# Decoder block: four-pair scans, placement copies on ScalarE, fewer VectorE steps per table, longer rows in the first loads

## Chip, cores and metric

The kernel runs on one core of one Trainium2 chip. The metric is device time in microseconds of one execution; a kernel is timed in several runs, and the median of the three runs before the change is 398.58 us (397.07 to 398.76). The engines are named as the profile names them: PE is TensorE (matmuls), PEld its weight loads, DVE is VectorE, ACT is ScalarE, POOL is GpSimd and SP is the queue from which all loads of weights are issued.

## The reference

One layer of a decoder block over 256 tokens of width 1024, in float32. Two branches run in parallel on the same projections: block-sparse attention (with a block of 256 tokens it is plain causal attention over 8 heads of 64) and an S5 diagonal state-space branch. Both are gated, summed, projected and normalized, and a convolutional gated FFN with a second normalization follows.

```python
proj = h @ w_in[l]                                  # q, k, v, u, g_attn, g_ssm
q, k = apply_partial_rotary(q), apply_partial_rotary(k)
attn = moba_attention(q, k, v)
ssm = s5_branch(u, a_re, a_im, log_dt, b_re, b_im, c_re, c_im, d, w_glu)
merged = sigmoid(g_attn) * (attn @ w_attn_proj) + sigmoid(g_ssm) * (ssm @ w_ssm_proj)
h = layer_norm(ALPHA * h + merged @ w_out, ln1_g, ln1_b)
val, gate = split(causal_depthwise_conv(h @ w_up, conv_w, conv_b))
h = layer_norm(ALPHA * h + (gelu(gate) * val) @ w_down, ln2_g, ln2_b)
```

The S5 branch has 32 groups of 16 channels with 64 complex states each. With `dt = exp(log_dt)` the state decays by `lb = exp(a * dt)` per token:

```python
x = z * (b @ u)                      # z from lb, a: complex, per state
h[s] = lb * h[s - 1] + x[s]          # over 256 tokens
y = Re(c @ h) + d * u
y = gelu(y);  y = y * sigmoid(y @ w_glu)
```

## The kernel before

**Order.** The program first records every operation with its reads, its writes and an estimated cost (class Recorder, lines 100 to 281). It then plans the order of each engine's queue by a list schedule over these costs, forward and backward, and issues all operations in the order that the planner found best. Every engine works through its queue in that order. The cost of an instruction comes from its class (Vec line 284, Act 351, Pe 377, Dma 425); a DMA is reckoned at its bytes by 330 GB/s (line 431). So a change of any cost or operation can change the whole order.

**Weights.** Products run in a reduced float32 form, so each operand is split into a high and a low part. A chunk of 128 x 1024 weights (512 KB) is loaded from the SP queue into a ring of `raw` buffers (three at first; `ctab` and `stab` are added later, line 979). ACT copies the high part to `wh` (some of the buffers are `yhl`, `shl`, `athl`, `xh`), DVE subtracts it from `raw` and writes the low part `wl` (`split_to`, line 476). A product is then three matmuls: high x high, low x high, high x low (`three`, line 491). A `raw` buffer can be loaded again only when DVE has made the low part.

**Start.** Before the first weights PE runs 28 small matmuls on zeros. `x` comes transposed in pieces (`x_piece`, line 562) into `gt`; the four chunks of the u weights go in halves to `ctab`, `stab` and two parts of `el`, and PE multiplies them unsplit (lines 579 to 591), into the banks `u_acc`. `small` is a tensor of parameters, of which the first 48 columns come early. Then come the q, k, v chunks and 16 gate chunks.

**S5 constants.** On 128 x 16 tiles (states of two groups by 16 pairs of groups) DVE works out exponentials, sine and cosine by series that run as scans (lines 624 to 696), then `z`, the even powers and the squared decay `mag2`. Two consecutive tokens are taken as one step of 128 (`NCH`). `uc` holds u in even and odd tokens: 32 copies of 32 rows out of the PSUM banks (lines 699 to 705), half on ACT, half on DVE. `e_tilde` and `gamma` (lines 728 and 738) build the input and output operands `et` and `gm` out of two products each on 128 x 512, and a sum per half of 64 rows, which writes to interleaved columns. `toeplitz` (841) builds the part within a step, `tz`.

**Tables and scans.** The rotation of the state is taken out of the scan: `turn_parts` makes angles in turns, and `tables(un)` (line 777) for a unit of four pairs adds a coarse and a fine angle, takes away the nearest whole number, and takes a sine and, through the absolute value, a cosine on ACT. `ssm_unit` (line 866) then multiplies by the tables, scans with the real decay (a scan for each of four pairs, real and imaginary, lines 885 to 888) and multiplies back. `ssm_out` (896) makes the outputs and applies Gelu. The four units are interleaved with the four pairs of attention heads and the gates (lines 976 to 983).

**After it.** Projections of attention and S5 output, the GLU product, the output projection, the first normalization, then 22 blocks of the FFN (from line 1159) and the second normalization with the output.

Of the kernel before, what the change touches and what calls it, by code (L numbers as in the profile page):

```python
# [20 lines left out]
P = 128  # L21
# [53 lines left out]
def _free(ap):  # L75
    n = 1
    for d in ap.shape[1:]:
        n *= d
    return n
# [345 lines left out]
class Dma:  # L425
# [2 lines left out]

    def dma_start(self, o, a):
        sb_in, sb_out = a.space != bass.MemoryType.DRAM, o.space != bass.MemoryType.DRAM  # L430
        n = _free(o if sb_out else a) * P * 4
        self.rec.add("SP", lambda: self.real.dma_start(o, a), [o] if sb_out else [],  # L432
                     [a] if sb_in else [], 0.45, dur=n / 330e3)

# [1 line left out]
def block_kernel(ctx: ExitStack, tc: tile.TileContext, w, xtok, small, lnv, out):  # L438
# [73 lines left out]
    qk = Ring([sb(f"qk{i}", NH, DH) for i in range(2)])  # L512
    ra, rb = sb("ra", NH, 16), sb("rb", NH, 16)
    sa, sb_, sc, sd = (sb(n, 4, NCH) for n in ("sa", "sb", "sc", "sd"))
    sgr, sgi = sb("sgr", 4, NCH), sb("sgi", 4, NCH)
    ga, gb, gk = (sb(n, 4, NCH) for n in ("ga", "gb", "gk"))
    hri = [(sb(f"hr{i}", 4, NCH + 1), sb(f"hi{i}", 4, NCH + 1)) for i in range(2)]
# [27 lines left out]
        return sml[:, a:b]  # L545

    eye = col("eye")
    halfpi = sb("halfpi", 1)

    warm = sb("warm", P, dt=BF16)  # L550
    V.memset(warm, 0.0)
    G.memset(halfpi, math.pi / 2)


    late = [tuple(again(t[:, i], (1024,)) for i in range(2)) for t in (yhl, shl, athl)]
# [6 lines left out]
    def x_piece(k0, k1):  # L562
        SP.dma_start(again(xr, (KD * S,))[:, k0 * S:k1 * S], w[C_X + k0 // 4][:, k0 % 4 * S:((k1 - 1) % 4 + 1) * S])

    x_piece(0, 1)


    A.copy(xh[:, 0, 0:1], warm[:, 0:1])
# [9 lines left out]
    u_room = [again(ctab, (1024,)), again(stab, (1024,))] + [again(el[:, 4 * i:4 * i + 4], (1024,)) for i in range(2)]  # L578
    for kk in range(4):
        r = u_room[kk]  # L580
        for j, (n0, n1) in enumerate(((0, 512), (512, 1024))):
            SP.dma_start(r[:, n0:n1], w[C_U + kk][:, n0:n1])
            if kk == 0 and j == 0:
                x_piece(1, 2)
            elif kk < 3 and j == 1:
                x_piece(2 * kk + 2, 2 * kk + 4)
        if kk == 0:
            SP.dma_start(sml[:, 0:48], small[:, 0:48])
        for h in range(2):
            for m in range(4):  # L590
                u_sum[m].add(r[:, h * 512 + m * P:h * 512 + (m + 1) * P], xr[:, 2 * kk + h])
# [107 lines left out]
    for q in range(4):  # L699
        for i4 in range(4):  # L700
            i = 4 * q + i4
            for j in range(2):
                b0 = 64 * (i % 2) + 32 * j
                src = u_acc[q][32 * i4:32 * i4 + 32, j:S:2]
                (V.tensor_copy if q % 2 else A.copy)(uc[b0:b0 + 32, i // 2], src)

# [1 line left out]
        G.memset(et[ri], 0.0)  # L710
    G.memset(gm, 0.0)
    G.memset(tz, 0.0)
    for t in hri[0] + hri[1]:
        G.memset(t[:, :, 0:1], 0.0)

# [12 lines left out]
    def e_tilde(ri, t0, t1_):  # L728

        b0, b1, op = ((bre, bim, SU), (bim, bre, AD))[ri]  # L730
        a, b = again(t0, ikh), again(t1_, ikh)
        tt(a, bc_h(zz[:, 0::2, 0]), bc_k(b0), MU)
        tt(b, bc_h(zz[:, 0::2, 1]), bc_k(b1), MU)
        for g in range(2):
            r = slice(64 * g, 64 * g + 64)
            tt(et[ri][r, :, :, g], a[r], b[r], op)

    def gamma(ri):

        b0, b1 = ((cre, cim), (cim, cre))[ri]  # L740
        cc = (zz[:, 1::2], zn)[ri]
        a, b = again(ga, ikh), again(gb, ikh)
        tt(a, bc_h(cc[:, :, 0]), bc_k(b0), MU)
        tt(b, bc_h(cc[:, :, 1]), bc_k(b1), MU)
        for g in range(2):
            r = slice(64 * g, 64 * g + 64)
            tt(gm[r, ri, :, 1:3, g], a[r], b[r], AD if ri else SU)

    for g in range(2):
        r = slice(64 * g, 64 * g + 64)  # L750
# [11 lines left out]
    def turn_parts():  # L762
        tt(whole, cidx, bc_c(tau), MU)
        ts(whole, whole, MAGIC, AD, MAGIC, SU)
        tt(turns, cidx, bc_c(tau_h), MU)
        tt(part, cidx, bc_c(tau_l), MU)
        tt(turns, turns, whole, SU)
        tt(turns, turns, part, AD)


    b0 = _COLS["bre"][0]
# [5 lines left out]
    def tables(un):  # L777
        tab = slice(8 * (un // 2) + un % 2, 8 * (un // 2) + 8, 2)
        tt(again(ga, (4, 8, 16)), turns[:, tab, 0:8].unsqueeze(3).to_broadcast([P, 4, 8, 16]),
           turns[:, tab, 8:24].unsqueeze(2).to_broadcast([P, 4, 8, 16]), AD)  # L780
        ts(gk, ga, MAGIC, AD, MAGIC, SU)
        tt(ga, ga, gk, SU)
        ct, st = cs[un]
        A.activation(st, ga, AF.Sin, scale=6.283185)
        V.tensor_scalar(gk.bitcast(I32), ga.bitcast(I32), 0x7FFFFFFF, None, op0=ALU.bitwise_and)
        A.activation(ct, gk, AF.Sin, scale=-6.283185, bias=halfpi)

    turn_parts()
    tables(0)
    e_tilde(0, sa, sb_)  # L790
    e_tilde(1, ga, gb)
    gamma(0)
    gamma(1)
    tables(1)
    tables(2)

# [46 lines left out]
    def toeplitz(half):  # L843
        pt = s5()
        for mm in range(4):
            m = 4 * half + mm
            e = er()
            for ri in range(2):
                A.copy(e[:, ri], et[ri][:, 2 * m:2 * m + 2, 1].rearrange("p i g h -> p i (g h)")
                       .unsqueeze(2).to_broadcast([P, 2, 2, 32]))  # L850
            for ri in range(2):
                T.matmul(pt[:, mm * P:(mm + 1) * P], e[:, ri].rearrange("p i j c -> p (i j c)"),
                         gm[:, ri, 2 * m:2 * m + 2, 0:2].rearrange("p i m g h -> p i (m g h)"),
                         start=ri == 0, stop=ri == 1)
        pv = pt.rearrange("p (a i m c) -> p a i m c", a=4, i=2, m=2)
        ms = slice(4 * half, 4 * half + 4)
        for par in range(2):
            r0 = slice(64 * par, 64 * par + 32)
            r1 = slice(64 * par + 32, 64 * par + 64)
            tt(tz[r0, ms, 0:32], pv[r0, :, par, 0], di[r0, ms], AD)  # L860
            V.tensor_copy(tz[r0, ms, 32:64], pv[r0, :, par, 1])
            tt(tz[r1, ms, 32:64], pv[r1, :, par, 0], di[r1, ms], AD)

    y = again(et[0], (4, S))
# [1 line left out]
    def ssm_unit(un):  # L866

        big, par = un // 2, un % 2
        pairs = [8 * big + 2 * k + par for k in range(4)]
        r = slice(64 * par, 64 * par + 64)  # L870
        pe = [s5(), s5()]
        for ri in range(2):
            for k, i in enumerate(pairs):
                T.matmul(pe[ri][:, k * P:(k + 1) * P], el[r, i // 2, ri], uc[r, i // 2],
                         start=True, stop=True)
        er_, ei_ = (p.rearrange("p (a c) -> p a c", a=4) for p in pe)
        ct, st = cs[un]
        hr_, hi_ = hri[par]
        tt(sa, ct, er_, MU)
        tt(sd, st, er_, MU)  # L880
        tt(sb_, st, ei_, MU)
        tt(sc, ct, ei_, MU)
        tt(sa, sa, sb_, AD)
        tt(sc, sc, sd, SU)
        for src, dst in ((sa, sgr), (sc, sgi)):
            for k, i in enumerate(pairs):
                V.tensor_tensor_scan(dst[:, k], mag2[:, i:i + 1].to_broadcast([P, NCH]),
                                     src[:, k], 0.0, MU, AD)
        tt(ga, ct, sgi, MU)
        tt(gb, st, sgr, MU)  # L890
        tt(hi_[:, :, 1:], ga, gb, AD)
        tt(sa, ct, sgr, MU)
        tt(sb_, st, sgi, MU)
        tt(hr_[:, :, 1:], sa, sb_, SU)
# [375 lines left out]
```

## Time and profile before

| | us |
|---|---|
| median of three runs | 398.58 |
| profiled execution | 399.22 |
| its span in the trace | 397.1 |
| PE busy in the span | 378.6 |
| DVE busy | 325.3 |
| ACT busy | 225.2 |
| POOL busy | 7.0 |

The span runs from the first to the last instruction of the execution; the profiled execution's own time holds some 2 us around it. A busy share of an engine is an average over stages that have different limits. A busy PE is one that has a matmul in flight: records overlap, so the spacing of their starts tells how fast it works. In rows of a timeline, the numbers are the start, the time, the engine, the line, the operation, what it writes and reads, and the count of merged instructions; in brackets stands the idle time before it and what ended that. Nearly all DVE rows have line 295, all ACT rows 371 and all DMA issues 432, as those are the lines of the recording helpers, so the tiles tell them apart.

### The profile page before, as it was taken

The numbers are of one execution on the slowest core, as the hardware profiler recorded it, in microseconds if no ns is written. First come the engines' busy times: TensorE is split into PE (matmuls) and PEld (weight loads), VectorE is DVE, ScalarE is ACT, GpSimd is POOL, SyncE is SP. The second block draws the span as 40 slices with busy tenths as digits, with TensorE's granted clock in tenths as the row PEclk, the third lists the DMA queues.
The fourth block names the chain that finished last, engine by engine and source line by source line (L and its number), as shares of the span: only waits on it lengthen the run. The fifth ranks groups of instructions, "written<-read, shape, count | busy, mean of one in ns | idle before, by whom it ended". The sixth has DMA issues, their size and how long they took to land.

```text
span 397.1 us, 6974 instructions
## 1 busy us (share of the span) xinstructions
PE 378.6 (95%) x2668; PEld 341.8 (86%) x2668; DVE 325.3 (82%) x636; ACT 225.2 (57%) x405; POOL 7.0 (2%) x47
## 2 busy tenths in 40 slices
PE   9898999999999999999799999999999999999980
PEld 8676787899798989988799999999999999999960
DVE  3899999899889967987988997777777677776666
ACT  3476585764897549724427756565665656555400
POOL 6000000000000000000000000000000000000000
PEclk9999999999999999999989999999999999999996
DMA  7814506364811663578327776554556555552002
GB/s 209 354 53 158 194 19 210 110 210 155 273 54 54 214 213 106 200 267 301 135 65 269 249 227 210 205 206 163 196 177 211 186 189 179 193 194 71 2 0 106
DMA packets 19905, 67.36 MB, mean 170 GB/s; under 512 B 2336, under 2 KB 2848, under 8 KB 19872
## 3 DMA queue, kind: packets, MB, share of 16 engines
q1 hardware_dynamic: 19872, 66.91, 49.3%
q8 instruction: 21, 0.34, 0.4%
q14 instruction: 12, 0.10, 0.1%
HBM read 65.86 MB, written 1.05 MB: 168 GB/s over the span
## 4 chain that ended last, share of the span: by engine, by line
PE 78%; DVE 14%; DMA 3%; issue 2%; SPq 1%; ACT 1%; DVEq 0%; ACTq 0%
PE bank L390 68%; PE bank L409 5%; DVE gm L295 3%; PE bank L416 3%; DMA ctab<-w 2%; DVE wl L295 2%; DMA gt<-w 2%; PE bank L422 1%; DVE uc L295 1%; DVE st L295 1%; DVE ty L295 1%; SPq L432 1%; DVE xl L295 1%; DVE ga L295 1%; DVE et L295 1%
## 5 line engine op out<-in xcount | busy, mean ns | idle before, releaser
L295 DVE TENSOR_TENSOR wl<-raw,wh 128x1024 fp32r<-128x1024 f32 x52 | 63.0, 1219 | 5.3 <-ACT wh L371 5.2
L295 DVE SCALAR_TENSOR_TENSOR qk<-bank,sml,qk 128x255 f32<-128x255 f32 (+1 forms) x88 | 41.5, 480 | 29.1 <-ACT qk L371 27.8
L371 ACT ACTIVATE wh<-raw 128x1024 fp32r<-128x1024 f32 x52 | 54.3, 1053 | 17.1 <-PE bank L390 15.3
L371 ACT ACTIVATE qk<-bank,sml 128x256 f32<-128x256 f32 x44 | 24.6, 565 | 57.7 <-PE bank L390 57.7
L390 PE MATMUL bank<-shl,wh 128*128 128x256 f32 x320 | 45.6, 279 | 0.0
L390 PE MATMUL bank<-yhl,wh 128*128 128x256 f32 x288 | 41.5, 279 | 0.0
L390 PEld LDWEIGHTS bank<-shl,wh 128*128 128x128 f32 x320 | 40.9, 188 | 0.0
L390 PEld LDWEIGHTS bank<-yhl,wh 128*128 128x128 f32 x288 | 37.7, 188 | 0.8
L390 PE MATMUL bank<-yhl,wl 128*128 128x256 f32 x272 | 37.8, 278 | 0.0
L390 PEld LDWEIGHTS bank<-yhl,wl 128*128 128x128 f32 x272 | 34.3, 188 | 0.0
L390 PE MATMUL bank<-wh,athl 128*128 128x512 f32 x96 | 30.5, 396 | 0.0
L390 PE MATMUL bank<-xh,athl 128*128 128x512 f32 x80 | 24.4, 392 | 0.0
L390 PE MATMUL bank<-wh,xh 128*128 128x512 f32 (+1 forms) x80 | 21.0, 360 | 1.1 <-ACT wh L371 1.0
L390 PE MATMUL bank<-shl,xh 128*128 128x256 f32 (+1 forms) x112 | 19.9, 301 | 1.4 <-DVE shl L295 1.2
L390 PEld LDWEIGHTS bank<-wh,athl 128*128 128x128 f32 x96 | 17.6, 189 | 3.4
L390 PE MATMUL bank<-wh,xl 128*128 128x512 f32 (+1 forms) x80 | 19.6, 351 | 0.0
L390 PE MATMUL bank<-wl,athl 128*128 128x512 f32 x48 | 19.0, 395 | 0.0
L390 PE MATMUL bank<-yhl,xh 128*128 128x256 f32 (+1 forms) x112 | 18.9, 302 | 0.0
L390 PEld LDWEIGHTS bank<-shl,xh 128*128 128x128 f32 x112 | 15.8, 191 | 2.9 <-DVE shl L295 1.9
L390 PE MATMUL bank<-wl,xh 128*128 128x512 f32 (+1 forms) x80 | 18.0, 351 | 0.0
L295 DVE TENSOR_TENSOR wl<-stab,wh 128x1024 fp32r<-128x1024 f32 x14 | 17.1, 1219 | 0.8 <-ACT wh L371 0.8
L295 DVE TENSOR_TENSOR wl<-ctab,wh 128x1024 fp32r<-128x1024 f32 x14 | 17.1, 1220 | 0.6 <-ACT wh L371 0.6
(225 smaller groups left out, 785.9 us busy)
## 6 DMA issues: line engine op xcount, KB each, us to landing
raw<-w SPq DMA_DIRECT2D x74, 512.0 KB, 3.4
ctab<-w SPq DMA_DIRECT2D x19, 512.0 KB, 3.9
stab<-w SPq DMA_DIRECT2D x19, 512.0 KB, 3.3
gt<-lnv SPq DMA_DIRECT2D x4, 512.0 KB, 6.3
el<-w SPq DMA_DIRECT2D x4, 256.0 KB, 6.8
el<-xtok SPq DMA_DIRECT2D x2, 512.0 KB, 4.3
sml<-small SPq DMA_DIRECT2D x1, 800.0 KB, 7.3
gt<-w SPq DMA_DIRECT2D x3, 256.0 KB, 6.3
```

Source lines behind the costliest of these rows:

```text
L295: self.rec.add(self.eng, lambda: f(o, *args, **kw), [o], ins, self.base + more + n * rate)
L371: self.rec.add("ACT", lambda: f(o, a, func, **kw), outs, ins, cost, func=func.name)
L390: self.pe.real.matmul(self.o, l, r, start=self.done == 0, stop=self.done == self.n - 1)
L409: self.rec.add("PE", lambda: self.real.matmul(o, l, r, start=start, stop=stop), [o], [l, r], 4 * n / 2400 + 0.005)
L416: self.real.matmul(o, l, r, start=start, stop=stop)
L422: self.rec.add("PE", lambda: self.real.transpose(o, a, eye), [o], [a, eye], 0.109)
L432: self.rec.add("SP", lambda: self.real.dma_start(o, a), [o] if sb_out else [], [a] if sb_in else [], 0.45, dur=n / 330e3)
```

## The change

Five parts, and the planner's estimate of a DMA:

- The planner reckons a DMA by its row length: 128/16 rows by the larger of 0.06 us and 0.027 us + 0.0415 us per KB.
- `x` comes in pieces of two k-tiles (2 KB rows), each ahead of the chunk of u weights that uses it; before, the first two pieces had one k-tile each. The first columns of `small` now come fourth.
- The 16 copies of u that DVE made go to ACT, as do the four copies of `tz`.
- `e_tilde` and `gamma` add or subtract the two products at full width in place, and ACT copies the halves to their columns. `gamma` uses other scratch tiles.
- The angles get half a turn added, and one DVE instruction (is the sum at least 1, minus the sum) takes the place of rounding and subtracting. ACT makes the absolute value (`Abs`) that was a bit operation on DVE.
- A tile `mg` holds the decay for all four pairs of a unit in a row, filled by an ACT copy, with a zero in each pair's first column, so that one scan of 512 columns runs over four pairs; two scans for a unit instead of eight.

```diff
     def dma_start(self, o, a):
         sb_in, sb_out = a.space != bass.MemoryType.DRAM, o.space != bass.MemoryType.DRAM
-        n = _free(o if sb_out else a) * P * 4
+
+        row = _free(o if sb_out else a) * 4 / 1024
         self.rec.add("SP", lambda: self.real.dma_start(o, a), [o] if sb_out else [],
-                     [a] if sb_in else [], 0.45, dur=n / 330e3)
+                     [a] if sb_in else [], 0.45, dur=P / 16 * max(0.06, 0.027 + 0.0415 * row))
...
+    mg = sb("mg", 4, NCH)
...
-    halfpi = sb("halfpi", 1)
+    halfpi, onepi, point5 = sb("halfpi", 1), sb("onepi", 1), sb("point5", 1)
+    G.memset(point5, 0.5)
...
-    G.memset(halfpi, math.pi / 2)
+    G.memset(halfpi, -math.pi / 2)
+
+    G.memset(onepi, 3.1415925)
...
-    x_piece(0, 1)
+    x_piece(0, 2)
...
-        for j, (n0, n1) in enumerate(((0, 512), (512, 1024))):
-            SP.dma_start(r[:, n0:n1], w[C_U + kk][:, n0:n1])
-            if kk == 0 and j == 0:
-                x_piece(1, 2)
-            elif kk < 3 and j == 1:
-                x_piece(2 * kk + 2, 2 * kk + 4)
+        if kk:
+            x_piece(2 * kk, 2 * kk + 2)
+        for h in range(2):
+            SP.dma_start(r[:, h * 512:(h + 1) * 512], w[C_U + kk][:, h * 512:(h + 1) * 512])
...
-                (V.tensor_copy if q % 2 else A.copy)(uc[b0:b0 + 32, i // 2], src)
+                A.copy(uc[b0:b0 + 32, i // 2], src)
...
+    G.memset(mg[:, :, 0:1], 0.0)
...
         tt(a, bc_h(zz[:, 0::2, 0]), bc_k(b0), MU)
         tt(b, bc_h(zz[:, 0::2, 1]), bc_k(b1), MU)
+        tt(a, a, b, op)
         for g in range(2):
             r = slice(64 * g, 64 * g + 64)
-            tt(et[ri][r, :, :, g], a[r], b[r], op)
-
-    def gamma(ri):
+            A.copy(et[ri][r, :, :, g], a[r])
+
+    def gamma(ri, t0, t1_):
...
+        tt(a, a, b, AD if ri else SU)
         for g in range(2):
             r = slice(64 * g, 64 * g + 64)
-            tt(gm[r, ri, :, 1:3, g], a[r], b[r], AD if ri else SU)
+            A.copy(gm[r, ri, :, 1:3, g], a[r])
...
-        tt(turns, turns, part, AD)
+
+        stt(turns, turns, 0.5, part, AD, AD)
...
-        ts(gk, ga, MAGIC, AD, MAGIC, SU)
-        tt(ga, ga, gk, SU)
+
+        stt(ga, ga, 1.0, ga, ALU.is_ge, SU)
         ct, st = cs[un]
-        A.activation(st, ga, AF.Sin, scale=6.283185)
-        V.tensor_scalar(gk.bitcast(I32), ga.bitcast(I32), 0x7FFFFFFF, None, op0=ALU.bitwise_and)
-        A.activation(ct, gk, AF.Sin, scale=-6.283185, bias=halfpi)
+        A.activation(st, ga, AF.Sin, scale=6.283185, bias=onepi)
+        A.activation(gk, ga, AF.Abs, bias=point5)
+        A.activation(ct, gk, AF.Sin, scale=6.283185, bias=halfpi)
...
-    gamma(0)
-    gamma(1)
+    gamma(0, sc, sd)
+    gamma(1, sgr, sgi)
...
-            V.tensor_copy(tz[r0, ms, 32:64], pv[r0, :, par, 1])
+            A.copy(tz[r0, ms, 32:64], pv[r0, :, par, 1])
...
+
+        A.copy(mg[:, :, 1:], mag2[:, pairs[0]:pairs[-1] + 1:2].unsqueeze(2).to_broadcast([P, 4, NCH - 1]))
         for src, dst in ((sa, sgr), (sc, sgi)):
-            for k, i in enumerate(pairs):
-                V.tensor_tensor_scan(dst[:, k], mag2[:, i:i + 1].to_broadcast([P, NCH]),
-                                     src[:, k], 0.0, MU, AD)
+            V.tensor_tensor_scan(dst.rearrange("p k c -> p (k c)"), mg.rearrange("p k c -> p (k c)"),
+                                 src.rearrange("p k c -> p (k c)"), 0.0, MU, AD)
```

More of the change, by code (lines that the diff above doesn't have):

```diff
@@ L733, in e_tilde @@
         tt(b, bc_h(zz[:, 0::2, 1]), bc_k(b1), MU)
+        tt(a, a, b, op)
         for g in range(2):
             r = slice(64 * g, 64 * g + 64)
-            tt(et[ri][r, :, :, g], a[r], b[r], op)
-    def gamma(ri):
+            A.copy(et[ri][r, :, :, g], a[r])
+    def gamma(ri, t0, t1_):
         b0, b1 = ((cre, cim), (cim, cre))[ri]
         cc = (zz[:, 1::2], zn)[ri]
-        a, b = again(ga, ikh), again(gb, ikh)
+        a, b = again(t0, ikh), again(t1_, ikh)
         tt(a, bc_h(cc[:, :, 0]), bc_k(b0), MU)
         tt(b, bc_h(cc[:, :, 1]), bc_k(b1), MU)
+        tt(a, a, b, AD if ri else SU)
         for g in range(2):
             r = slice(64 * g, 64 * g + 64)
-            tt(gm[r, ri, :, 1:3, g], a[r], b[r], AD if ri else SU)
+            A.copy(gm[r, ri, :, 1:3, g], a[r])
     for g in range(2):
```

## The prediction

> **What bounds the kernel now.** The page's shares are averages over stages, so I read busy time by stages first and then the chain that ended last.
>
> ```profile
> 0.00:20.00 20.00, 17.59 (x85) 14.43 (x86) 11.90 (x66) 8.00 (x16) 6.64 (x38) 1.00 0.81 280
> 20.00:48.00 28.00, 25.57 (x114) 19.43 (x113) 27.27 (x54) 18.06 (x36) 0.00 (x0) 1.00 0.38 131
> 48.00:66.00 18.00, 18.00 (x113) 15.45 (x112) 17.45 (x42) 13.12 (x29) 0.00 (x0) 1.00 0.27 93
> 66.00:170.00 104.00, 104.00 (x861) 93.49 (x861) 91.67 (x187) 72.43 (x160) 0.37 (x9) 1.00 0.49 165
> 170.00:200.00 30.00, 27.56 (x175) 24.76 (x174) 25.31 (x49) 12.12 (x15) 0.00 (x0) 0.97 0.62 219
> ```
>
> After the stretch and its length the columns are PE, PEld, DVE, ACT and POOL, then granted clock, DMA share and GB/s. In 20 to 48 us DVE is busy 27.27 of 28 us and PE has holes. From 48 to 170 us PE is never idle, though DVE is nearly full as well. The chain says the same: it runs through DVE until 47.6 us and then through PE.
>
> ```profile
> 46.31 1.24 DVE shl L295
> 47.59 1.43 PE bank L390 x5
> ...
> 147.63 23.02 PE bank L390 x196
> ...
> 201.70 179.11 PE bank L390 x1298
> ```
>
> So the change can save only what PE loses before about 48 us: PE's own work from there on is untouched, and what follows PE's last matmul is the second normalization and the output, which the diff doesn't touch either. How much PE loses, from PE's timeline:
>
> ```profile
> 11.58 1.30 PE L390 MATMUL bank<-gt,el 128*128 128x256 f32 x4 [0.69 <-DMA el<-w]
> 13.61 1.28 PE L390 MATMUL bank<-gt,el 128*128 128x256 f32 x4 [0.74 <-DMA el<-w]
> 14.73 1.89 PE L390 MATMUL bank<-gt,stab 128*128 128x256 f32 x8
> 20.85 1.08 PE L390 MATMUL bank<-yhl,xl 128*128 128x512 f32 x4
> 21.77 1.08 PE L390 MATMUL bank<-yhl,xh 128*128 128x512 f32 x4
> 30.06 1.20 PE L390 MATMUL bank<-shl,xh 128*128 128x512 f32 x4 [0.86 <-DVE shl L295]
> 34.96 0.74 PE L390 MATMUL bank<-wh,xh 128*128 128x512 f32 x2 [0.99 <-ACT wh L371]
> 47.59 0.73 PE L390 MATMUL bank<-shl,xh 128*128 128x512 f32 x2 [0.38 <-DVE shl L295]
> ```
>
> In the u product PE waits 0.69 + 0.74 = 1.43 us for a transfer, while eight records of stab that it runs only at 14.73 (1.89 us) read another chunk. In the q and k products four wide records follow each other in 21.77 - 20.85 = 0.92 us, 0.23 each. The stretch 20 to 48 holds 114 records; by its grouped rows, 93 of them are wide (93 x 0.23 = 21.4), 9 are of u (1.89/8 = 0.236 each, 2.1) and 12 are transposes.
>
> ```profile
> 20.00:48.00 28.00, 1.91 (x12) 1.33 (x12) 1.00 0.38 131
> 20.00:48.00 28.00, 2.29 (x9) 1.50 (x8) 0.00 (x0) 0.60 (x1) 1.00 0.38 131
> ```
>
> These are the 12 of line 422 and the 9 that read el. Counting the transposes at their busy mean, 1.91/12 = 0.16, and thus too high if anything, gives 1.9, so PE's work is 25.4 us at most; at half a wide record (0.115) it is 24.9. I take 24.9 and a loss of 28 - 24.9 = **3.1 us**. The Trainium skill ("Trainium Kernel Development and Optimization", Performance Expectations) says that matmul busy time is a poor measure because matmuls are pipelined. The trace agrees: busy time shows only 28 - 25.57 = 2.43 us; by that the sum below would end 0.5 us higher.
>
> Why DVE is late: with DVE full, the splits that free the weight buffers are late, the SP queue waits for them, and no byte moves from 22 to 30 us.
>
> ```profile
> 22.00:30.00 8.00, 7.21 (x32) 5.63 (x30) 7.64 (x17) 5.00 (x10) 0.00 (x0) 1.00 0.00 0
> ```
>
> ```profile
> SPq L432 <- DVE wl L295: 111.6, 49, 11.7
> ```
>
> **The change part by part.** DVE's groups that it touches (busy, mean ns):
>
> ```profile
> L295 DVE COPY uc<-bank 32x128 f32<-32x128 f32 x16 | 4.6, 286 | 0.3
> L295 DVE TENSOR_TENSOR ga<-ga,gk 128x512 f32<-128x512 f32 x4 | 2.7, 686 | 0.1
> L295 DVE TENSOR_SCALAR gk<-ga 128x512 f32<-128x512 f32 x4 | 1.7, 425 | 0.2
> L295 DVE TENSOR_SCALAR gk<-ga 128x512 int32<-128x512 int32 x4 | 1.7, 420 | 0.0
> L295 DVE TENSOR_TENSOR gm<-ga,gb 64x512 f32<-64x512 f32 x4 | 2.7, 681 | 0.0
> L295 DVE COPY tz<-bank 32x128 f32<-32x128 f32 x4 | 1.1, 282 | 0.0
> L295 DVE TENSOR_TENSOR_SCAN sgr<-ty,sa 128x128 f32<-128x128 f32 x16 | 6.2, 405 | 0.0
> L295 DVE TENSOR_TENSOR_SCAN sgi<-ty,sc 128x128 f32<-128x128 f32 x16 | 5.6, 399 | 0.0
> L295 DVE TENSOR_TENSOR_SCAN sd<-sc,sgr 128x256 f32<-128x256 f32 x1 | 0.7, 665 | 0.0
> ```
>
> *Copies of u*: 16 leave DVE, 4.6 us, all before 48 us. *Halves of et and gm*: four pairs of 64-row sums become four full-width sums; a 64-row one costs as much per instruction as a full one, so 4 x 0.68 = 2.7 us go, of which three pairs (2.0) lie before 48. *Tables*: per table 0.425 + 0.686 + 0.420 become one compare-and-subtract, which I price as the 128x512 sum, 0.686 (bounds: 0.42 as the fast forms here, and twice 0.686): 0.84 saved, four times 3.4, one of them before 48. *tz*: 1.1. *Scans*: 32 of 128 columns take 11.8. From 128 (0.405) to 256 (0.665) a scan grows by 0.260, so one of 512 takes about 0.665 + 2 x 0.260 = 1.19 and eight 9.5; 2.3 saved (bounds: 0.665, the longest scan in the trace, saving 6.5; and four short ones, 1.62, losing 1.2). The last addition of the angles only changes its form (0). In all DVE loses about 14 us, **7.4 of them (4.6 + 2.0 + 0.84) before 48 us**.
>
> ACT takes them. The nearest rows:
>
> ```profile
> L371 ACT ACTIVATE uc<-bank 32x128 f32<-32x128 f32 x16 | 4.3, 267 | 0.2
> L371 ACT ACTIVATE gm<-sml 64x256 f32<-64x256 f32 x4 | 1.7, 414 | 1.0 <-DMA sml<-small 1.0
> L371 ACT ACTIVATE ctab<-gk,halfpi 128x512 f32<-128x512 f32 x2 | 1.5, 726 | 0.2 <-DVE gk L295 0.2
> L371 ACT ACTIVATE stab<-ga 128x512 f32<-128x512 f32 x2 | 1.3, 632 | 0.0
> L371 ACT ACT_TABLE_LOAD x6 | 7.7, 1283 | 0.8 <-PEq L1262 0.7
> ```
>
> Before 48 us: 16 x 0.267 = 4.3 for u; six half copies, each between 0.41 (half the columns) and 0.63 (the same columns), I take 0.6, 3.6; one Abs 0.7. That is 8.6 us, beside ACT's idle 28 - 18.06 = 9.9. Behind these copies on ACT's queue stand the high halves of the weights, for which PE waits; this is the cover that can fail, and the slower rival below prices it. After 48: two half copies, three Abs with the longer bias of both sines, four copies of tz and four of the decay rows, 1.2 + 2.5 + 1.1 + 2.5 = 7.3 us, beside 18 - 13.12 = 4.9 idle until 66 us and 104 - 72.43 = 31.6 after it. I cost them at nothing: until 170 us PE has other products to run, as its 104.00 of 104 shows with DVE as full as it was. The scan now waits for the decay copy on ACT; behind it on DVE stand the splits of the weights. That copy depends on mag2 alone, so it can go ahead at any time after the previous unit's scan; without that cover it costs one copy, 0.63 us, per unit. POOL gets three more memsets at the start, beside 20 - 6.64 = 13 idle us (0).
>
> *First transfers*: x comes in four pieces instead of five, in front of the chunk that uses it, and the small parameters go fourth instead of sixth. One issue goes:
>
> ```profile
> gt<-w SPq DMA_DIRECT2D x2, 128.0 KB, 2.5
> ctab<-w SPq DMA_DIRECT2D x2, 256.0 KB, 3.2
> ```
>
> A first piece twice as long lands up to 3.2 - 2.5 = 0.7 us later, but the second half of chunk 0 has no more bytes ahead of it than before, and the 1.43 us of waiting for el is later still; so 0. The later bytes are the same, with the DMA engines at a share of 0.81 until 20 us, so they land no earlier. But the planner now reckons 0.88 us (8 x (0.027 + 0.0415 x 2)) instead of 0.79 for such a half chunk, and 0.48 instead of 0.07 for the small one, so it should place ready work ahead of late work: PE's eight stab records in the waits for el, and DVE's small steps ahead of this one:
>
> ```profile
> 11.28 0.42 DVE L295 TENSOR_TENSOR xl<-gt,xh 128x256 fp32r<-128x256 f32 x1 [2.25 <-ACT xh L371]
> ```
>
> I take 0.9 of the 1.43 us for PE (bounds 0 and 1.43).
>
> **The sum.** With 7.4 us less on DVE, its 27.27 falls to 19.9 of PE's 24.9, so PE would set this stage. What is late next is ACT (18.06 + 8.6 = 26.7) and the transfers. I take two thirds of the 3.1, 2.1 us (bounds 0 and 3.1). From 48 us on 0, but the whole order is planned anew; one misplaced wait costs what the longest PE waits above cost, about 1.0 us either way. Together 0.9 + 2.1 = **3.0 us**. The profiled execution took 399.22 (span 397.1), 0.64 above the median 398.58. It should become 396.2, span 394.1; against the median, **395.6 us**.
>
> **Rivals.** *ACT takes DVE's place, slower.* The mechanism is a weight's high half queued behind copies of u, et and gm between 20 and 48 us. ACT's DMA waits there,
>
> ```profile
> ACT shl L371 <- DMA raw<-w: 1.7, 1, 1.7
> ACT wh L371 <- DMA raw<-w: 1.3, 1, 1.3
> ```
>
> may stay, 3.0 us, if buffers aren't freed earlier. Then ACT needs 26.7 + 3.0 = 29.7 for 28 us, and if nothing is put off the stage grows by 1.7; with one misplaced wait of 1.0 and no gain in u this gives 401.3. It decides once over 9.9 - 3.0 = 6.9 us of copies must run before PE can go on. Against it: those waits come from DVE's late splits, ACT also stood 5.7 us waiting for et, and the gm copies can go behind 48 us. *No change*: PE's holes move to other operands, as its order has one fixed queue; 398.4. For it: one hole of 0.99 is ACT's already. *All holes close*: 1.43 + 3.1, 394.0. *Abs forces table loads*: Abs between two sines would reload twice per table, 8 x 1.283 = 10.3 us of ACT, 2.6 of it before 48; 26.7 + 2.6 = 29.3 of 28, and 7.7 beside 4.9 idle until 66, together 4.1 on top of the forecast without its 2.1: 401.8. Against it: the six loads of before show that Copy between sines brings none. The Trainium skill ("ScalarE: Activation LUTs", Table sets: the hidden batching unit) has abs in every set as filler, so none here; no run shows Abs yet. That the change doesn't do what it says I see only in the planner, under no change.
>
> **How the numbers follow.** Forecast 0.51; all holes close 0.13; no change 0.24; ACT late 0.09; table loads 0.03. The range goes from all holes closed and 1.0 better order, 398.58 - 4.5 - 1.0 = 393.0, to no gain and 1.0 worse, 399.6; the two slower rivals (0.12) and the tails lie outside. About 0.5% (2.0 us) is what a measurement of this kernel can tell from no change: faster needs under 396.6. Of the forecast about 0.03 lies above it: faster 0.51 - 0.03 + 0.13 = 0.61, same 0.27, slower 0.12.
>
> **What would show it.** Right: PE without idle from about 45 us or earlier; DVE under 22 us in 20 to 48; bytes moving in 22 to 30 us; eight scans of about 1.2 us; still six table loads; the step from PE's last product to the end unchanged. Wrong: PE waits on ACT's wh growing before 66 us, table loads above six, stab still behind el, or PE idle appearing after 66 us.

## The result and the profile after

The changed kernel takes 391.89 us (391.42 to 392.07), beside 398.67 us of the kernel before in the same runs: a ratio of 0.9833, 95% interval 0.9801 to 0.9865. The direction was right. The saving, 6.8 us, is more than twice the forecast 3.0, and the time lies below the range. Of all the executions below, three took 470 to 624 us at a granted clock of 0.56 to 0.75 and are left out of every ratio and count.

The busy time by stages of the changed kernel (columns as in the prediction):

```profile
0.00:20.00 20.00, 17.94 (x89) 15.19 (x90) 13.92 (x63) 9.25 (x26) 6.73 (x41) 1.00 0.82 292
20.00:48.00 28.00, 26.37 (x126) 20.87 (x125) 24.08 (x43) 27.39 (x54) 0.00 (x0) 1.00 0.43 142
48.00:66.00 18.00, 17.96 (x101) 14.90 (x100) 15.82 (x29) 17.36 (x36) 0.00 (x0) 1.00 0.60 204
66.00:170.00 104.00, 104.00 (x878) 95.07 (x877) 89.54 (x165) 73.41 (x166) 0.37 (x9) 1.00 0.44 150
170.00:200.00 30.00, 28.58 (x209) 26.75 (x208) 25.93 (x53) 11.49 (x14) 0.00 (x0) 1.00 0.55 186
```

From 20 to 66 us ACT is now the fullest engine (27.39 of 28 and 17.36 of 18), as forecast (26.7). DVE has 24.08 there, not 19.9: if 7.4 us went, as reckoned, 4.2 of other work moved in. From 48 to 66 us transfers run at 204 GB/s instead of 93.

The products of the changed kernel on the chain that ended last (start, time), and below them the last S5 outputs of the kernel before:

```profile
139.26 3.81 PE bank L416 x48
...
194.20 179.44 PE bank L390 x1298
```

```profile
143.82 3.81 PE bank L416 x48
```

The last S5 outputs come 4.56 us earlier, and the 1298 products of the FFN start 201.70 - 194.20 = 7.50 us earlier and take as long as before. So all of the gain lies ahead of 194 us, and most of it behind 48 us, where I had costed nothing.

To place it I take every matmul of a trace in order, give it the spacing of its kind in an undisturbed row (0.229 us for 512 columns, 0.115 for 256, and so on), and note how far PE lags behind the sum of this work. The sums are equal in both kernels (358.9 us), so the lags can be subtracted even where the order differs:

| us of lag gained | before | after | difference | forecast |
|---|---|---|---|---|
| up to work 16 (about 23 us, u product) | 7.60 | 6.73 | -0.87 | -0.9 |
| 16 to 36 (to about 46 us) | 3.35 | 2.73 | -0.62 | -2.1 |
| 36 to 60 (to about 72 us) | 2.90 | 0.96 | -1.94 | 0 |
| 60 to 150 (to about 167 us) | 5.03 | 4.19 | -0.84 | 0 |
| 150 to 178 (to about 199 us, output projection, normalization) | 5.55 | 2.34 | -3.21 | 0 |

The border at work 36 lies just ahead of the kernel before's wait that ends at 47.59, so this wait, with 0.65 us of lag, is counted in the third row. Put with the second, where the forecast had it, the second row gains 1.3 and the third 1.3. Ahead of 48 us the change thus gains 2.1 us, and behind it 5.4. In both traces PE's clock is at full from 7.0 us on, so the first rows can be compared.

PE's timeline of the changed kernel shows the first two rows:

```profile
9.27 2.75 PE L390 MATMUL bank<-gt,stab 128*128 128x256 f32 x12
...
13.61 1.28 PE L390 MATMUL bank<-gt,el 128*128 128x256 f32 x4 [0.72 <-DMA el<-w]
14.73 0.59 PE L390 MATMUL bank<-gt,stab 128*128 128x256 f32 x2
...
26.62 0.52 PE L422 MATMUL bank<-sml,et 128*128 128x128 f32 x3 [1.12 <-issue]
27.66 0.96 PE L390 MATMUL bank<-wh,xh 128*128 128x512 f32 x3 [0.52 <-ACT wh L371]
```

Twelve records of stab now run ahead of the wait for el, and one of the two waits is gone. Much of the gain in the next stage is eaten by a new hole at 25.5 to 27.7 us, which ACT's timeline explains:

```profile
21.61 1.10 ACT L371 ACTIVATE uc<-bank 32x128 f32<-32x128 f32 x4
22.73 1.28 ACT L371 ACT_TABLE_LOAD   x1
24.02 0.72 ACT L371 ACTIVATE stab<-ga,onepi 128x512 f32<-128x512 f32 x1
24.65 0.71 ACT L371 ACTIVATE gk<-ga,point 128x512 f32<-128x512 f32 x1
25.27 1.25 ACT L371 ACTIVATE et<-sa 64x512 f32<-64x512 f32 x2
26.55 1.06 ACT L371 ACTIVATE wh<-raw 128x1024 fp32r<-128x1024 f32 x1
```

The high half `wh`, for which PE waits, stands behind u copies, a table load, the table and the copies of et: the mechanism of the slower rival, here for about 2 us.

For the rows behind 46 us, the same stretch of PE's timeline, first before, then after:

```profile
66.97 0.40 PE L390 MATMUL bank<-wh,xl 128*128 128x512 f32 x1
67.30 0.92 PE L409 MATMUL bank<-kT,qT 64*128 64x128 f32 x4
68.14 0.96 PE L390 MATMUL bank<-wh,xl 128*128 128x512 f32 x3
68.94 0.63 PE L390 MATMUL bank<-wl,xh 128*128 128x512 f32 x2
69.50 0.92 PE L409 MATMUL bank<-kT,qT 64*128 64x128 f32 x4
70.35 0.73 PE L390 MATMUL bank<-wl,xh 128*128 128x512 f32 x2
71.01 0.48 PE L409 MATMUL bank<-uc,el 64*128 64x128 f32 x2
```

```profile
64.45 1.07 PE L390 MATMUL bank<-wl,xh 128*128 128x512 f32 x4
65.46 1.16 PE L409 MATMUL bank<-uc,el 64*128 64x128 f32 x8
66.45 0.93 PE L409 MATMUL bank<-kT,qT 64*128 64x128 f32 x8
67.31 2.17 PE L390 MATMUL bank<-xh,yhl 128*128 128x256 f32 x16
```

Before, the small products of 64 rows (attention scores, S5 inputs) come in several short batches between wide ones; after, they stand in one. PE counts as busy throughout. Yet after one wide product of 0.23 us the first kT record starts at 67.30, 0.33 after 66.97: 0.1 us is lost at the break inside a busy PE. As much again is lost one record later: the three wide records from 68.14 to 68.94 take 0.80 us, where three of 0.23 take 0.69.

Between work 36 and 140 (about 48 to 155 us), counted over the starts of all records, the kernel before has 32 breaks between products of 64 and of 128 rows, which cost 6.6 us, and the changed one 25, which cost 5.1; the alternations within the S5 outputs, 12 and 13, are left out. So the breaks are nearly all of what PE loses there, and 1.5 us of what the change saves. Of these breaks 26 and 13 are next to wide products; in the changed kernel 12 others are next to small products of 128 rows, where the kernel before has 6.

Finally the first normalization, before and after:

```profile
193.72 1.95 PE L409 MATMUL bank<-sa,gm 128*128 128x128 f32 x16
...
198.02 3.68 PE L409 MATMUL bank<-sb,gm 128*128 128x128 f32 x16 [2.35 <-DVE sb L295]
```

```profile
192.15 2.05 PE L409 MATMUL bank<-sb,gm 128*128 128x128 f32 x16 [1.42 <-DVE sb L295]
```

PE waits 0.93 us less for the second half, and the same 16 records take 2.05 us instead of 3.68; in the kernel before the granted clock is at half from 198.15 to 201.56 us.

### The profile page after: what moved, and what is told of

Its sections match the earlier page's. It is cut to its first block, busy times and chain, and to the rows that moved or that the text cites. A ratio compares the mean times of both kernels' runs of the same rounds, so it can differ in the third digit from the quotient of the medians.

```text
span 389.8 us, 6960 instructions
## 1 busy us (share of the span) xinstructions
PE 373.5 (96%) x2668; PEld 339.9 (87%) x2668; DVE 316.1 (81%) x580; ACT 238.7 (61%) x441; POOL 7.1 (2%) x50
## 4 chain that ended last, share of the span: by engine, by line
PE 88%; DVE 5%; ACT 3%; DMA 2%; SPq 1%; issue 1%; DVEq 0%; ACTq 0%
PE bank L390 78%; PE bank L409 5%; PE bank L416 3%; DVE gm L295 3%; DMA el<-w 2%; PE bank L422 2%; ACT uc L371 1%; SPq L433 1%; DVE st L295 1%; ACT L371 0%; ACT et L371 0%; ACT wh L371 0%; ACT shl L371 0%; ACT yhl L371 0%; DVE sc L295 0%
## 5 line engine op out<-in xcount | busy, mean ns | idle before, releaser
L295 DVE TENSOR_TENSOR athl<-qk,athl 128x256 fp32r<-128x256 f32 x22 | 9.3, 424 | 13.9 <-ACT athl L371 13.9
L390 PE MATMUL bank<-wh,xh 128*128 128x512 f32 (+1 forms) x80 | 20.0, 354 | 0.5 <-ACT wh L371 0.5
L371 ACT ACTIVATE wh<-stab 128x1024 fp32r<-128x1024 f32 x14 | 14.7, 1053 | 4.7 <-DMA stab<-w 2.7
L390 PEld LDWEIGHTS bank<-yhl,xh 128*128 128x128 f32 x112 | 16.1, 190 | 1.3
```

Source lines behind the costliest of these rows:

```text
L295: self.rec.add(self.eng, lambda: f(o, *args, **kw), [o], ins, self.base + more + n * rate)
L371: self.rec.add("ACT", lambda: f(o, a, func, **kw), outs, ins, cost, func=func.name)
L390: self.pe.real.matmul(self.o, l, r, start=self.done == 0, stop=self.done == self.n - 1)
```

## The experiments

Theories at first: the freed DVE and the busier ACT do it by themselves (then single parts add up); or the planner's order does, because any change makes it choose anew. A third, that the planner's choice between its own candidates does it, came late, and the last two runs test it. Ratios are to the kernel before in the same set of runs, with 95% intervals. "Wait" is a parameter of the planner explained further on.

| run | wait | median us | ratio |
|---|---|---|---|
| changed kernel | 0.4 | 391.89 | 0.9833 (0.9801 to 0.9865) |
| e1_plan | 0.2 | 399.05 | 1.0026 (1.0003 to 1.0049) |
| e2_scan | 0.2 | 403.71 | 1.0154 (1.0114 to 1.0194) |
| e3_act | 0.4 | 395.24 | 0.9933 (0.9907 to 0.9960) |
| e4_tables | 0.2 | 400.53 | 1.0070 (1.0041 to 1.0100) |
| e5_before_2ns | 0.2 | 398.47 | 1.0026 (1.0007 to 1.0045) |
| e6_after_2ns | 0.4 | 392.17 | 0.9861 (0.9819 to 0.9903) |
| e7_fill | 0.2 | 397.56 | 0.9984 (0.9966 to 1.0003) |
| e8_after_oldplan | 0.4 | 392.64 | 0.9871 (0.9840 to 0.9902) |
| e9_after_uc_dve | 0.2 | 396.86 | 0.9983 (0.9956 to 1.0010) |
| e10_after_old_scan | 0.4 | 392.28 | 0.9855 (0.9814 to 0.9896) |
| e11_after_old_tables | 0.4 | 391.00 | 0.9834 (0.9796 to 0.9871) |
| e12_uc | 0.2 | 397.61 | 1.0010 (0.9979 to 1.0041) |
| e13_etgm | 0.2 | 400.45 | 1.0064 (1.0043 to 1.0085) |
| e14_after_place_only | 0.4 | 392.02 | 0.9865 (0.9833 to 0.9896) |
| e16_after_et0_direct | 0.2 | 397.40 | 0.9971 (0.9940 to 1.0001) |
| e17_before_wait04 | 0.4 | 396.14 | 0.9960 (0.9945 to 0.9974) |
| e18_after_wait02 | 0.2 | 397.53 | 0.9993 (0.9974 to 1.0012) |

### One part alone on the kernel before: e1 to e4

Each takes lines of the change alone: the estimate of a DMA, the scans with `mg`, the three placements on ACT, the tables.

```diff
e1
+                     [a] if sb_in else [], 0.45, dur=P / 16 * max(0.06, 0.027 + 0.0415 * row))
e2
+            V.tensor_tensor_scan(dst.rearrange("p k c -> p (k c)"), mg.rearrange("p k c -> p (k c)"),
e3
+                A.copy(uc[b0:b0 + 32, i // 2], src)
+            A.copy(et[ri][r, :, :, g], a[r])
+            A.copy(gm[r, ri, :, 1:3, g], a[r])
+            A.copy(tz[r0, ms, 32:64], pv[r0, :, par, 1])
e4
+        stt(ga, ga, 1.0, ga, ALU.is_ge, SU)
+        A.activation(gk, ga, AF.Abs, bias=point5)
```

> The kernel before with only the planner's estimate of a DMA changed; no instruction differs, only the order. Theory 'freed engine time' (the saving comes from the work taken off DVE): at most the 0.9 us of the u product, 397.5 to 398.7. Theory 'new order' (any edit plans the whole order anew, and what it does to the holes after 48 us and to the wait between the two halves of the first normalization decides): off 398.7 by more than 1 us either way, with a different wait between the two groups of sixteen transposes (2.35 us before) and with or without the half clock at 198 to 201.6 us.

> The kernel before with only the scans over four pairs. 'Freed engine time': about 2.3 us less of DVE after 64 us; PE was said to be full there, so 398.2 to 398.7; if PE's small losses in 48 to 140 us do come from DVE, 397.0 to 398.0. 'New order': anywhere from 396 to 400, decided at the first normalization.

> The kernel before with only the copies of u and tz and the placement of et and gm on ACT. 'Freed engine time': 6.6 us less DVE before 48 us, so 396.0 to 397.5 if ACT isn't late; if ACT is late at 20 to 30 us (a high half of the q weights behind the copies, as the changed kernel's trace shows near 25 to 28 us), 398.5 to 400. 'New order': decided at the first normalization, 1.6 us by the clock and 1.1 us by a split placed inside it.

> The kernel before with only the tables in fewer DVE steps and Abs on ACT. 'Freed engine time': 0.84 us before 48 us and 2.5 after, 397.5 to 398.5, with six table loads; eight or more loads would mean that Abs needs one. 'New order': off by more than 1 us either way through the first normalization.

Only the placements are faster, by 0.67%; scans and tables alone are slower, though both take work off DVE. Two runs lie outside what was expected: e3 is faster than the first theory allowed, and e2 slower than either. Each has a low granted clock in all its executions (0.983 to 0.987 and 0.979 to 0.982); in the traces it is at half from 25.64 to 29.05 us in e3, and in e2 from 11.64 to 15.06 and from 35.54 to 38.95. The four single ratios multiply to 1.018, the whole is 0.983. So these parts do not add up (the first transfers weren't run alone), and less work on DVE does not pay by itself.

### Is it any order? e5, e6, e8

DVE's fixed cost in the planner is raised by 2 ns, in both kernels, and the changed one gets the old estimate of a DMA back.

```diff
e5, e6
-    eng, unit, base = "DVE", 1.04e-3, 0.066
+    eng, unit, base = "DVE", 1.04e-3, 0.068
e8
-                     [a] if sb_in else [], 0.45, dur=P / 16 * max(0.06, 0.027 + 0.0415 * row))
+                     [a] if sb_in else [], 0.45, dur=n / 330e3)
```

> The kernel before with every DVE cost in the planner 2 ns higher; the instructions are the same, only their order may differ. 'Freed engine time': 398.7 within 0.6. 'New order': off by 1 us or more, with other waits at 20 to 48 us and in the first normalization.

> The changed kernel with every DVE cost in the planner 2 ns higher. 'Freed engine time': 391.9 within 0.6. 'New order': 392 to 396, back by up to 2.7 us if the clock drops in the first normalization or a split falls inside it, and by the ACT hole at 25 to 28 us if that goes the other way.

> The changed kernel with the planner's old estimate of a DMA (bytes by 330 GB/s). 'Freed engine time': 391.9 plus at most the 0.9 us of the u product, 392.8. 'New order': 393 to 397 with other waits in the first normalization.

Each kernel stays within 0.4% of its own ratio. So it isn't a lottery at every change, and the new estimate isn't needed for the gain.

### The normalization: e7

Ten idle products fill PE's wait between the two halves; nothing reads them.

```diff
+        for i in range(10 if t == 0 else 0):
+            T.matmul(S5[2][:, 0:P], sx[:, 0, 0:P], dg[0], start=True, stop=True)
```

> The kernel before with ten more matmuls of PE (twenty records, 2.2 us at full clock) between the two halves of the first normalization, whose result nobody reads. If the half clock at 198 to 201.6 us comes from PE's 2.35 us of idle before it, the second sixteen transposes take 2.0 us instead of 3.68 and the kernel 396.8 to 397.6. If the clock drop has another cause, the transposes stay at 3.7 and the time at 398.7 or above. The order is planned anew here too, so the trace of that place decides, not the time alone.

The granted clock by window, first of the kernel before, then with the filler (time, PE busy, clock, DMA share, GB/s):

```profile
198.00:202.00 4.00, 3.98 (x20) 0.57 0.28 103
```

```profile
198.00:202.00 4.00, 4.00 (x36) 1.00 0.37 135
```

The drop to half clock is gone in this trace, but the median gains only 0.16%, and the interval reaches 1. That is not because the drop is rare. It lowers the mean granted clock of an execution, which is 0.986 in the profile before and 0.991 in that of the changed kernel, where there is no drop. In the five sets of runs from e1 on, 63 of 105 executions of the kernel before have a mean of 0.987 or lower, with a median of 398.36 us; the other 42 have 0.990 or higher, and a median of 396.91. That it is this same drop in all 63 is not shown, since only one of this kernel's executions was traced; e1 and e5, with nearly the same time, have theirs at 199.4 to 203 us. With the filler 3 of 10 are still at 0.988 or lower, and the other seven have a median of 397.56, not below the 397.11 of the kernel before's nine executions at 0.989 or higher in the same set: what the filler saves in clock it seems to cost again.

So the 1.6 us of the drop (3.68 - 2.05), part of the 3.21 in the table above, belong to most executions of the kernel before, and one of the four of the changed kernel has a low mean (0.986). Against the 396.91 the changed kernel's 391.89 is a gain of 5.0 us; between one and two of the 6.8 are the clock.

### Undoing one part of the changed kernel, and halves of the placement: e9 to e14, e16

```diff
e9, and reversed on the kernel before in e12
-                A.copy(uc[b0:b0 + 32, i // 2], src)
+                (V.tensor_copy if q % 2 else A.copy)(uc[b0:b0 + 32, i // 2], src)
e10, and in e14
-            V.tensor_tensor_scan(dst.rearrange("p k c -> p (k c)"), mg.rearrange("p k c -> p (k c)"),
...
+            for k, i in enumerate(pairs):
+                V.tensor_tensor_scan(dst[:, k], mag2[:, i:i + 1].to_broadcast([P, NCH]),
e11, and in e14
-        stt(ga, ga, 1.0, ga, ALU.is_ge, SU)
+        ts(gk, ga, MAGIC, AD, MAGIC, SU)
+        tt(ga, ga, gk, SU)
e13, on the kernel before; reversed for et alone in e16
+        tt(a, a, b, op)
-            tt(et[ri][r, :, :, g], a[r], b[r], op)
+            A.copy(et[ri][r, :, :, g], a[r])
```

> The changed kernel with the eight pairs of u copies back as before, half on ACT and half on DVE. Theory 'ACT late' (the hole of 2 us at 25 to 28 us is the weights' high half behind u copies, and is all that the move of these copies costs): the hole shrinks by over 1 us and the kernel takes 390.0 to 391.3. Theory 'u copies are the gain' (DVE before 48 us is what bounds PE, and these are its largest part there, 4.6 us): 394 to 397, with DVE above 26 us busy in 20 to 48 us and PE waiting for low halves.

> The changed kernel with the scans pair by pair. If parts that free DVE after 60 us matter beside the others, 392.9 to 394 with more breaks between kinds of matmul at 60 to 140 us; if the placement on ACT brings nearly all, 391.5 to 392.6.

> The changed kernel with the tables made as before (rounding, subtraction and bit operation on DVE). If the tables matter beside the others, 392.9 to 394.5; if the placement on ACT brings nearly all, 391 to 392.6, the Abs being off ACT near the hole at 25 us.

> The kernel before with only the 16 copies of u moved to ACT. Theory 'u copies are the gain': 395 to 396.5, as the whole placement gave (395.2). Theory 'et and gm are the gain' (full-width sums, and copies in between): 397.5 to 399.

> The kernel before, with only the sums of et and gm made at full width on DVE and placed in halves by ACT (the u copies stay shared, tz, scans, tables, first transfers and planner as before). Theory 'both placements together': this one alone stays near the kernel before, 396 to 399 us (ratio 0.995 to 1.00), with the many breaks between kinds of matmul (70 or more switches between 55 and 165 us), as the u copies alone did. Rival 'et and gm alone do it': 394 to 395.5 us, as with all three placements, and under 60 switches.

> The changed kernel with the pair-by-pair scans and the old table angles put back together, so that the placements on ACT, the first transfers and the planner's estimate are all that is left of the change. Theory 'placement and start are all': 390.5 to 393 us, within 0.4% of the changed kernel. Rival 'scans or tables are needed, either will do': taking both away costs what neither cost alone, 395 us (the placements alone on the kernel before) or more.

> The changed kernel with the halves of et written by DVE directly as before (gm and u stay on ACT). ACT has four copies of about 1.2 us less ahead of the high half wh for which PE waits at 27 us. Theory 'ACT is late there': the hole of 25.3 to 27.7 us shrinks by 1 us or more and the kernel takes 390 to 391.5 us if the later order stays in the good family. Rival 'the placement on ACT is needed as a whole': 394 us or more, with 65 or more switches.

Scans and tables can both be taken back and the gain stays (e10, e11, e14). Take back half of the u copies (e9) or the copies of et (e16), and all but 0.2 or 0.3% is gone; either placement alone (e12, e13) gains nothing. e16 speaks against work as the cause: its DVE is freer from 20 to 48 us than in the changed kernel, 22.81 of 28 us beside 24.08, and the median is nearly that of before. (Half of its ten executions have a mean clock of 0.986 or 0.987 and a median of 398.4 us, half one of 0.991 or 0.992 and 394.9; even the latter are 3 us above the changed kernel.)

```profile
20.00:48.00 28.00, 26.36 (x123) 20.98 (x122) 22.81 (x40) 27.31 (x60) 0.00 (x0) 1.00 0.42 135
48.00:66.00 18.00, 17.40 (x99) 13.59 (x98) 15.30 (x35) 17.63 (x42) 0.00 (x0) 1.00 0.42 133
```

### What a break costs: e15

Behind the last products stand four blocks, each of 64 wide matmuls (fp32r, 256 columns) and 64 small fp32 ones of 128 columns, in runs of 32 and then of 4; small ones of 64 rows in the first two blocks, of 128 in the last two. Their results go nowhere.

```diff
+        for small in ((qT[0:64, 0, 0:P], kT[0:64, 0, 0:P]), (qT[:, 0, 0:P], kT[:, 0, 0:P])):
+            block(small, [32, 32])
+            block(small, [4] * 16)
```

> The kernel before with four blocks of matmuls behind the last products, each of 64 wide ones (fp32r, 128 rows, 256 columns) and 64 small fp32 ones of 128 columns, once in runs of 32 and once in runs of 4; in the first two blocks the small ones have 64 rows, in the last two 128 rows. Their results go nowhere. Theory 'a change of kind costs PE time': a block in runs of 4 takes 28 x 0.1 us or more longer than its block in runs of 32, 2.8 us (each block about 14 us), perhaps in one direction only. Rival 'the breaks are waits for operands that the trace does not show': both blocks take the same time within 0.3 us. If only 64-row ones pay, the rows and not the type are the cause.

The windows cut at the blocks' starts (time, PE busy, clock, DMA share, GB/s):

```profile
385.31:407.94 22.63, 22.63 (x193) 1.00 0.13 47
407.94:435.99 28.05, 28.05 (x193) 1.00 0.01 1
435.99:457.98 21.98, 21.98 (x193) 1.00 0.00 1
457.98:479.80 21.82, 21.82 (x194) 1.00 0.01 2
```

With 64 rows, 28 more breaks take 28.05 - 22.63 = 5.42 us, 0.19 each; with 128 rows nothing. PE is "busy" in all of it. So a change between products of 64 and of 128 rows costs PE time by itself, as much as the two steps of 0.1 us in the kernel, and a change of type doesn't. (The expectation says some 14 us a block; an fp32 matmul is two records of 0.115, so a block takes 22.)

### The planner's choice: e17, e18

The planner doesn't make one order. It makes 40: two directions, four rounds, and five values of `wait`, the share of an operation's cost that an engine will stand idle for a more urgent operation. It takes the shortest by its own model:

```python
for from_end in (False, True):
    ...
    for r in range(rounds):
        for wait in (0.0, 0.2, 0.4, 0.6, 0.8):
            end = self.forward(key, wait)
            ...
            if best is None or end < best[0]:
                best = (end, [o.start for o in self.ops])
```

Which wait it chose stands in the table above, and it parts the runs. Until then all seven kernels with 0.4, the changed one among them, had taken 391.0 to 395.2 us, and all with 0.2 took 396.9 to 403.7. By its model the choice hardly matters: for the changed kernel 386.12 us with 0.4 and 386.53 with 0.2; for the kernel before 386.44 with 0.2, 388.79 with 0.4. The last two runs force the other choice of wait.

The wait is not all that parts the runs. In the seven kernels with 0.4 the planner took a plan of its first direction, whose first key is the order of recording. With 0.2 it took one of that direction in the kernel before, e5 and e7, and one of the other direction, planned from the end, in e1, e2, e4, e9, e12, e13 and e16. e17 keeps the first direction, so it differs from the kernel before in the wait alone; e18's plan is one from the end, so it differs from the changed kernel in both. The changed kernel's best plan of the first direction with 0.2 (386.85 us by the model) wasn't run.

```diff
e17 (kernel before); e18 is the same line with 0.2 in the changed kernel
-                    if best is None or end < best[0]:
+                    if wait == 0.4 and (best is None or end < best[0]):
```

> The kernel before, computing exactly what it did; only its planner may choose no plan but those in which an engine waits up to 0.4 of an operation's cost for a more urgent one (before it took one with 0.2, by its own model 2.4 us the shorter). Theory 'the gain behind 48 us is the chosen wait': the breaks in the middle fall to about 60, the lost time there from 7.3 to 5 or 6 us, and the kernel takes 394 to 396.5 us without any of the change. Rival 'the longer wait only pays once DVE has been relieved': 398 to 402 us, as the planner's model has it.

> The changed kernel, whole; only its planner may choose no plan but those with a wait of 0.2 (it took one with 0.4; by its own model the other is 0.4 us longer). Theory 'the chosen wait': 65 or more breaks again, 394.5 to 397.5 us, that is the forecast of 395.6 or so, since what is left is the gain ahead of 48 us. Rival 'the freed DVE is what saves the time behind 48 us, whatever the wait': 391.5 to 393 us.

The changed kernel with an order of 0.2 gains nothing: 0.9993 (0.9974 to 1.0012). The kernel before with an order of 0.4 gains 0.40%, at the slow end of what the first theory allowed. Together they give 1.67%, so neither theory holds by itself: the gain needs the change and the order that the planner chose for it. The clock doesn't alter this: the executions with a mean of 0.989 or higher have 396.13 us in e17 and 397.02 in e18, beside 397.18 of the kernel before in the same set. Whether the wait or the direction makes the changed kernel's order the better one isn't separated, and each of the four cases is a single order. The lag of PE, in the stages of the first table:

| us of lag gained at work | up to 16 | 16 to 60 | 60 to 150 | 150 to 178 |
|---|---|---|---|---|
| before, 0.2 | 7.60 | 6.25 | 5.03 | 5.55 |
| before, 0.4 (e17) | 9.14 | 6.54 | 4.56 | 2.21 |
| changed, 0.2 (e18) | 4.77 | 8.21 | 6.25 | 3.29 |
| changed, 0.4 | 6.73 | 3.69 | 4.19 | 2.34 |

The first column holds the start, where the clock differs: it is at full from 7.0 us on in the first and last, from 5.4 in e18, and from 3.8 in e17, where it is at half again from 14.06 to 17.48. The others speak of the order. From work 16 to 60 the change saves 2.9 us with the orders of 0.4 (6.54 to 3.69) and loses 2.0 with those of 0.2 (6.25 to 8.21). PE's timeline of e18 shows why:

```profile
22.61 1.19 PE L390 MATMUL bank<-shl,xh 128*128 128x512 f32 x4 [0.88 <-ACT shl L371]
29.42 0.97 PE L390 MATMUL bank<-wh,xh 128*128 128x512 f32 x3 [0.79 <-ACT wh L371]
33.87 1.18 PE L422 MATMUL bank<-sml,et 128*128 128x128 f32 x9 [1.04 <-ACT et L371]
36.34 0.51 PE L390 MATMUL bank<-wh,xh 128*128 128x512 f32 x1 [0.85 <-ACT wh L371]
50.31 1.16 PE L409 MATMUL bank<-gm,er 128*128 128x128 f32 x8 [0.99 <-ACT er L371]
```

Five waits on ACT, 4.55 us: what was taken off DVE (21.92 of 28 us busy there, as forecast) is paid back on ACT. And with the old load on DVE the order of 0.4 loses time in front too: e17's PE waits 1.55 us for DVE and is busy only 16.04 of 18 us at 48 to 66 us, with DVE at 26.00 of 28 just ahead.

```profile
49.49 0.71 PE L390 MATMUL bank<-wh,xh 128*128 128x512 f32 x2 [1.55 <-DVE rb L295]
```

```profile
20.00:48.00 28.00, 27.14 (x120) 21.12 (x118) 26.00 (x51) 16.93 (x33) 0.00 (x0) 1.00 0.38 123
48.00:66.00 18.00, 16.04 (x104) 14.00 (x105) 15.08 (x34) 13.49 (x30) 0.00 (x0) 1.00 0.54 173
```

The breaks do not follow the wait alone, though the expectation said so: between 64 and 128 rows there are 30 in e17 (6.1 us) and 32 in e18 (7.0), beside 32 (6.6) before and 25 (5.1) in the changed kernel's own order. No kernel here beats the changed one clearly: e11, 391.00 us, has the same ratio.

## Why the prediction was wrong

**The start: right.** 0.9 us forecast in the u product, 0.87 found, by stab's records moved into the wait for el: one wait of two is gone, as the rows show.

**The q and k products: right in kind, too large.** "I take two thirds of the 3.1, 2.1 us": 1.3 came up to 48 us. DVE was freed, but "What is late next is ACT" was priced at a third of the stage's loss, 1.0 us, and ACT, at 27.39 of 28, made a hole of about 2. Bytes moved from 22 to 30 us, but only at 39 GB/s.

```profile
22.00:30.00 8.00, 6.37 (x31) 4.69 (x29) 7.47 (x12) 7.83 (x15) 0.00 (x0) 1.00 0.13 39
```

**Behind 48 us: this step failed.** "So the change can save only what PE loses before about 48 us", and in the sum "From 48 us on 0", with 1.0 us either way for the order. It came to 5.4 us in the profile. The nothing rested on PE's 104.00 busy of 104. But a busy PE was losing time: 32 breaks between 64 and 128 rows at 0.2 us each from 48 to 155 us, of which the changed kernel's order takes away 1.5 us. Nor did it hold behind 170 us, where the prediction's own row shows PE busy only 27.56 of 30 us and a clock of 0.97, both priced at nothing: there 0.93 us of waiting and the 1.6 of the clock drop went. And the order as a whole is worth far more than 1.0 us: the same changed kernel takes 397.53 us in one of the planner's orders and 391.89 in another. With e18's order the forecast would have been too fast by 1.9 us; with the planner's choice it was too slow by 3.7. I had the planner's change of order as a nuisance of 1.0 us on a sum of engine times; together with the change it was the main term.

**What cost nothing: right.** Scans, tables and tz were costed at nothing, and taking scans and tables back changes nothing (e14, 0.9865 beside 0.9833, intervals overlapping). Their prices were right as well: a scan of 512 columns was to take 1.19 us, and there are still six table loads, so Abs brings none.

```profile
L295 DVE TENSOR_TENSOR_SCAN sgi<-mg,sc 128x512 f32<-128x512 f32 x4 | 4.9, 1213 | 0.0
L295 DVE SCALAR_TENSOR_TENSOR ga<-ga 128x512 f32<-128x512 f32 x4 | 2.8, 690 | 0.1
```

```profile
L371 ACT ACT_TABLE_LOAD x6 | 7.7, 1283 | 0.8 <-PEq L1270 0.7
L371 ACT ACTIVATE gk<-ga,point 128x512 f32<-128x512 f32 x4 | 2.8, 711 | 0.0
```

**The rivals.** ACT late is real: 2 us of it in the changed kernel, 4.55 in e18, whose time is that of "no change". Which of the two happens was decided by 0.41 us in the planner's model.

**What stays open.** Why the model sees 0.4 us between orders that are 5.6 us apart on the chip. The cost of a break of 64 rows isn't in its costs (e18's breaks cost 1.9 us more than the changed kernel's), nor, it seems, is how late ACT is in front; a planner with these costs wasn't tried. Nor is it shown whether the wait or the direction of the plan matters, or why both placements are needed for the planner to choose 0.4: only that in every kernel without one of them it chose 0.2.

## What to carry to other kernels

Where a program plans its own order, a change is two changes: the work, and the order that the planner now picks. Measure them apart, by holding the planner's choice still on both kernels, before believing that the removed work paid, and try its runners-up on the chip, since a model's difference of 0.1% may be 1.4% there. And an engine that is busy all the time isn't thereby working at full rate: compare the spacing of its instructions with that of an undisturbed run.

## What was not expected of the hardware

A change between matmuls of 64 and of 128 rows costs about 0.2 us, in a row of alternations (0.19) as in the kernel (6.6 us for 32), inside time that the profile counts as busy; in the kernel's rows half of it comes at the break and half one record later. Between fp32 and fp32r of 128 rows a change costs nothing that can be seen.

PE's clock fell to half (0.57 in the window row of 198 to 202 us) after PE had waited 2.35 us once. With ten idle products in the gap it stayed at 1.00 in the trace. The Trainium skill ("TensorE: Matmul & The Clock Gate", HAM oscillation) warns of idle gaps above some 3.4 us. Here a shorter one was enough in the traced execution; three fifths of the kernel before's executions have a mean clock as low as this one's.
